# Wide projections, attention outcome in groups of four query tiles, and the recurrence's values by way of DRAM, in a one-core hybrid block

## The chip, the cores and the metric

The kernel runs on one core of one Trainium2 chip. The metric is the device time of one execution in microseconds, from a few runs of the same kernel; lower is better. The change is looked at against the kernel before, run on the same chip.

## What is computed

One layer of a streaming encoder on 1024 tokens of width 1024, all in float32. Cut to what matters here:

```python
h = rmsnorm(x, norm_mix_g)
z = h @ w_in                                   # one projection, cut into:
(hq, hf, hi, hg, fq, fk, fv, ff, mq, gate_logits) = split(z)
y_a = hgrn2(hq, hf, hi, hg)                    # gated recurrence, 4 heads of 128, chunks of 64
y_b = fox(fq, fk, fv, ff)                      # attention, 8 heads of 64, causal, with forget bias
y_c = memory(mq, rmsnorm(mem) @ mem_kv_w)      # attention into 256 memory tokens, 4 heads of 128
gates = sigmoid(gate_logits)                   # one gate per branch and channel
merged = sum(gates[b] * (y @ w_br[b]) for b, y in enumerate((y_a, y_b, y_c)))
x = x + merged @ w_out
h2 = rmsnorm(x, norm_ffn_g)
a, v = split(h2 @ w_up)                        # 2 x 2816
x = x + (gelu(causal_conv3(a)) * v) @ w_down

# fox, per head and block of 128 queries, over all keys s <= t:
s = q_hat @ k_hat.T / 8 + F[t] - F[s]          # F: running sum of log forget gates
y = softmax(s) @ v                             # q_hat, k_hat: normed per head
```

## The kernel before, in words

**Precision.** Every product is made of three float32r matmuls (`mm3`, L158 to L162): a factor is split into a high part (a cast, L166) and the rest (a difference, L174), and high x high, high x low and low x high are added in PSUM. The attention's products with their own split operands use two (L924/L925 for the logits, L965/L966 for the outcome).

**Order of the work.** Nearly everything is laid out so that TensorE always has a matmul at hand. The program is written as generators that `weave` interleaves, and `ahead` gives the attention's and the recurrence's steps a higher priority, so that the scheduler takes other work ("fill") only where they are not ready. The order of each engine's instructions is fixed when the program is built; at run time an engine works through its own list and waits by semaphores. DMAs are issued from the queues of SyncE (SP) and of GpSimd (POOL), each in its order.

The stages by the span's time: norm and the normed input `uh`/`ul` (high and low), the dense units (gates, memory queries) up to about 212 us; values and keys/queries of the first attention pair, and the attention into memory, to 325; the forgetting attention to about 681; the recurrence (HGRN) to 895 with the branch of the attention; the other two branches to 980; output projection to 1070; channel mixer up to 1475 and its down projection to the end.

**The attention** has 4 pairs p of 2 heads i; head h is 2p + i. `fox_proj(p)` computes keys and queries of a pair by `token_major` (L704): 8 token tiles of 128, each one PSUM bank of which 256 columns are used, so 8 x 3 matmuls of 128x256 per tile (L160 to L162, `pp`). They go to a tile `z`, get their norm (squares, a reduction, a power on POOL) and are transposed by `fox_prep`. `fox_attn(p, i)` (L901) makes a head: it loads the head's forget bias as a row of 1024 to all partitions (`nf`, SP queue, L909), and takes query tiles two by two. For each query tile tb: logits (`lg`, two PSUM banks, up to 1024 keys), on DVE the bias added and the row maximum taken (L930; the diagonal tile with the masked bias `nfm` from POOL), small steps (L935 to L941), on ACT the exponential with its sum (L940), on POOL the scaling by the inverse sum (L942). Then the outcome of two query tiles: for each pair of key tiles the probabilities are transposed on PE (L953, L954, L956) into one of two banks `tr`, cast on ACT to `ph` (L166), the rest on DVE to `pl` (L174), and multiplied with the split values `vhl` (L965, L966) into `po`, of which 256 columns are used. `po` is evacuated by ACT and DVE to `yp` and stored (L969 to L971).

**The fill** beside each head: keys and queries of the next pair beside i = 0, gate chunks (`gates_early`) beside i = 1 (3, 3 and 3 of them by `NFOX`, one more beside the last pair), and the recurrence's values (`hgrn_values`, L1012) in two halves of 256 columns beside the last two heads, evacuated directly to `Vf`, which held the attention's values before. Behind the attention comes `hgrn_prep(0)`: six halves of 512 columns (`cm_chunk`), each evacuated by DVE (L1046) to a gate tile and on to the tiles of the recurrence. The scheduler takes it, too, between the last heads' steps.

**Buffers.** PSUM: three banks `pp` for projections, two `lg`, two `tr`, one `po`. Weights come to `raw` (2 buffers) and are split to `wh`, `wl` (3 buffers each). A gate tile is 128x512, from a small ring. The attention's row tiles `pt` have 4 buffers of 128x1024, which the squares of the key norm use as well.

## Time and profile before

| | us |
|---|---|
| runs of the kernel before | 1698.56, 1699.6, 1700.24 (median 1699.6) |
| profiled execution | 1700.23 |
| its span, first to last instruction | 1698.4 |
| PE busy | 1691.0 |
| DVE busy | 1150.8 |
| ACT busy | 800.9 |
| POOL busy | 324.6 |
| mean granted TensorE clock | 0.999 of full |

The profiled execution is one run; its span is what the rows of the profile add up to, and 1.8 us lie around it. A row such as `pp<-uh,wh 128x512 x205 | 80.9, 395` is a group of like instructions: how many, busy time and mean ns of one. Matmuls overlap in PE's pipeline, so that the distance of their starts is shorter than their length. In the timeline a row gives start, length, engine, line and tile. In the table of windows, each row gives the window, its length, then the busy time (and count) of PE, of PE's weight load, DVE, ACT and POOL, the granted clock, the DMA share and GB/s.

### The profile page before, as it was taken

Reading aid. Unit: us, or ns where it says so; the run is one execution under the profiler, and the core shown is the slowest. Engines: PE = TensorE matmul, PEld = TensorE weight load, DVE = VectorE, ACT = ScalarE, POOL = GpSimd, SP = SyncE. Lnnn points to the kernel's source line nnn. Section 1 sums busy time; section 2 is a strip of 40 time slices with the busy share of each in tenths; the row PEclk is TensorE's granted clock in tenths of the full one; section 3 lists DMA queues with packets and bytes.
Section 4 is the critical chain, followed back from the end, with each engine's and each line's share of the span. In section 5 each row is a group of like instructions: output and inputs, shape, how many; then the busy total and the mean of one; then the engine's idle time right before and its main releaser. Section 6 shows DMA issues by size and latency. Waiting matters only on the chain.

```text
span 1698.4 us, 24291 instructions
## 1 busy us (share of the span) xinstructions
PE 1691.0 (100%) x8957; PEld 1452.4 (86%) x8957; DVE 1150.8 (68%) x2057; ACT 800.9 (47%) x1428; POOL 324.6 (19%) x420
## 2 busy tenths in 40 slices
PE   9999999999999999999999999999999999999999
PEld 7888899989898998888888888888888888888887
DVE  6966455666666664886856845987878888775654
ACT  6734455545454553775631333644434444533432
POOL 0200032543433331544310000311111111100000
PEclk9999999999999999999999999999999999999999
DMA  9443232221212111110346542566544344494772
GB/s 367 157 161 106 88 139 68 77 92 51 94 59 77 63 46 57 67 32 13 106 127 209 167 186 100 165 174 169 158 139 138 118 149 143 172 363 145 251 269 87
DMA packets 83062, 227.16 MB, mean 134 GB/s; under 512 B 9712, under 2 KB 12408, under 8 KB 82816
## 3 DMA queue, kind: packets, MB, share of 16 engines
q1 hardware_dynamic: 64320, 160.54, 26.8%
q0 software_dynamic: 18048, 64.50, 13.2%
q8 instruction: 70, 1.15, 0.3%
q10 hardware_dynamic: 576, 0.59, 0.1%
q14 instruction: 48, 0.39, 0.1%
HBM read 180.72 MB, written 67.93 MB: 146 GB/s over the span
## 4 chain that ended last, share of the span: by engine, by line
PE 99%; DVE 0%; ACT 0%; DMA 0%; issue 0%; ACTq 0%; DVEq 0%
PE pp L160 21%; PE pp L162 21%; PE pp L161 21%; PE lg L160 4%; PE lg L162 4%; PE lg L161 4%; PE tr L162 3%; PE tr L161 3%; PE tr L160 3%; PE po L966 1%; PE lg L925 1%; PE lg L924 1%; PE po L965 1%; PE po L160 1%; PE po L161 1%; PE po L162 1%
## 5 line engine op out<-in xcount | busy, mean ns | idle before, releaser
L160 PE MATMUL pp<-uh,wh 128*128 128x512 f32 x412 | 163.3, 396 | 0.0
L161 PE MATMUL pp<-ul,wh 128*128 128x512 f32 x412 | 162.9, 395 | 0.0
L162 PE MATMUL pp<-uh,wl 128*128 128x512 f32 x412 | 162.5, 394 | 0.0
L161 PE MATMUL pp<-wl,uh 128*128 128x256 f32 (+1 forms) x512 | 146.3, 286 | 0.0
L162 PE MATMUL pp<-wh,ul 128*128 128x256 f32 (+1 forms) x512 | 146.1, 286 | 0.0
L160 PE MATMUL pp<-wh,uh 128*128 128x256 f32 (+1 forms) x512 | 145.6, 286 | 0.0
L166 ACT CAST wh<-s 128x512 fp32r<-128x512 f32 x110 | 66.5, 621 | 131.6 <-PE pp L161 55.1
L166 ACT CAST wh<-raw 128x1024 fp32r<-128x1024 f32 (+2 forms) x76 | 67.6, 890 | 100.6 <-PE pp L161 86.2
L166 ACT CAST wh<-rw 128x512 fp32r<-128x512 f32 x87 | 53.2, 619 | 108.1 <-PE pp L161 70.2
L160 PEld LDWEIGHTS pp<-wh,uh 128*128 128x128 f32 x512 | 97.3, 190 | 1.2
L161 PEld LDWEIGHTS pp<-wl,uh 128*128 128x128 f32 x512 | 97.4, 190 | 1.0
L162 PEld LDWEIGHTS pp<-wh,ul 128*128 128x128 f32 x512 | 97.4, 190 | 0.9
L1457 POOL DMA_DIRECT2D rw<-in_w_up x44 | 24.1, 555 | 372.4 <-DVE wl L1350 171.3
L166 ACT CAST dwh<-wr 128x1024 fp32r<-128x1024 f32 (+1 forms) x41 | 40.2, 980 | 115.8 <-PE tr L161 40.0
L162 PEld LDWEIGHTS pp<-uh,wl 128*128 128x128 f32 x412 | 77.5, 188 | 15.1
L174 DVE TENSOR_TENSOR wl<-raw,wh 128x1024 fp32r<-128x1024 f32 (+2 forms) x75 | 78.0, 1040 | 17.8 <-ACT wh L166 17.6
L160 PEld LDWEIGHTS pp<-uh,wh 128*128 128x128 f32 x412 | 77.5, 188 | 14.6
L161 PEld LDWEIGHTS pp<-ul,wh 128*128 128x128 f32 x412 | 77.5, 188 | 14.5
L940 ACT ACTIVATE pt<-pt,st 128x128 f32<-128x128 f32 (+3 forms) x64 | 49.7, 777 | 41.7 <-DVE st L937 33.9
L174 DVE TENSOR_TENSOR dwl<-wr,dwh 128x1024 fp32r<-128x1024 f32 (+1 forms) x41 | 46.3, 1129 | 31.7 <-ACT dwh L166 31.7
L942 POOL TENSOR_SCALAR pt<-pt,st 128x128 f32<-128x128 f32 (+3 forms) x64 | 49.1, 767 | 78.4 <-DVE st L941 64.1
L1350 DVE TENSOR_TENSOR wl<-rw,wh 128x512 fp32r<-128x512 f32 x69 | 47.7, 704 | 22.7 <-PE pp L162 18.2
(500 smaller groups left out, 5123.2 us busy)
## 6 DMA issues: line engine op xcount, KB each, us to landing
rw<-in_w_up POOLq DMA_DIRECT2D x44, 512.0 KB, 4.7
sd<-in_w_dn POOLq DMA_DIRECT2D x30, 512.0 KB, 6.0
br<-yd SPq DMA_DIRECT2D x30, 512.0 KB, 5.0
raw<-in_w_cm SPq DMA_DIRECT2D x24, 512.0 KB, 3.4
gd<-gt SPq DMA_DIRECT2D x48, 256.0 KB, 2.0
gt<-gd SPq DMA_DIRECT2D x48, 256.0 KB, 2.7
yd<-fc SPq DMA_DIRECT2D x44, 256.0 KB, 2.2
wr<-sd SPq DMA_DIRECT2D x20, 512.0 KB, 4.5
```

The source lines that it names most:

```text
L160: PE.matmul(ps, lh, rh, start=first, stop=False, skip_group_check=more)
L161: PE.matmul(ps, lh, rl, start=False, stop=False, skip_group_check=more)
L162: return PE.matmul(ps, ll, rh, start=False, stop=last, skip_group_check=more)
L166: return S.copy(out, in_)
L174: return (sub or V).tensor_sub(l, src, h.bitcast(F32))
L924: PE.matmul(ps[:, :w], qa[i][:, tsl], kh[i][:, s0:s0 + w], start=True, stop=False)
L925: fox_sets[p][3] = PE.matmul(ps[:, :w], qa[i][:, tsl], kl[i][:, s0:s0 + w], start=False, stop=True)
L940: S.activation(pt[:, :ns], pt[:, :ns], AF.Exp, bias=st[:, 2:3], accum_out=st[:, 3:4])
L942: G.tensor_scalar(pt[:, :ns], pt[:, :ns], st[:, 3:4], 0.0, ALU.mult, ALU.add)
L965: PE.matmul(o, vhl[:, sb, :], ph[:, src], start=(sb == 0), stop=False)
L1350: late["split"] = V.tensor_sub(l, src, h.bitcast(F32))
L1457: late["raw"] = G.dma_start(raw[:, 2 * i:2 * i + 2, :], src[:, 2 * i:2 * i + 2, :])
```

## The change

1. **Keys and queries of pairs 2 and 3 in one wide projection.** `fox_proj_late` projects 512 columns at a time (both pairs), evacuates them to a gate tile and stores them to DRAM (`zd`); `fox_load` loads each pair's part to `z` and does its norm. `w_late` replaces the last two parts of `w_fqk`.
2. **The recurrence's values** are projected 512 columns wide too and stored to DRAM (`hid`); 8 loads bring them to `Vf` behind the attention's last use of it.
3. **Outcome by groups of four query tiles.** For each key tile, up to four transposes fill one bank `tr`; one cast, one difference, and two matmuls of up to 512 columns. Row tiles `pt` are one tile per query tile, of the length it needs.
4. **Fill**: beside the heads now: pair 1's projection, 3 gates with one half of the wide projection, the other half with the load of pair 2, gates, load of pair 3, one gate and half of the values, the other half of the values.
5. **Squares in a tile of their own**, in halves.
6. **The last outcome's evacuation** (`fox_out` of head 7, group 1) is issued behind the third of the evacuations of `hgrn_prep(0)`, into a gate tile.
7. `wh` and `wl` have 4 buffers. The memory branch's eight loads (`yc`) are issued one by one through branch 0, each behind a small POOL instruction (`warm`) that reads a gate tile. In the channel mixer two loads move from POOL's queue to SP's, and two wait for POOL's differences. The program is built with a smaller DMA scratch (2048).

```diff
-NFOX = [0, 3, 0, 3, 0, 3, 1]
+NFOX = 10
+WIDE = 4
...
-            hl = [wp.tile([P, 4 * 264], F32R, tag=t, name=t, bufs=3) for t in ("wh", "wl")]
+            hl = [wp.tile([P, 4 * 264], F32R, tag=t, name=t, bufs=WIDE) for t in ("wh", "wl")]
...
-            w = [weights(src[q], (4, ncol)) for q in range(2)]
+            per = 2 if ncol == HB else 4
+            w = [weights(src[q], (per, ncol)) for q in range(KC // per)]
...
+    def fox_norm(z):
+        zz = z.rearrange("p b (h d) -> p (b h) d", d=64)
+        r = cp.tile([P, 16], F32, tag="fr", name="fr", bufs=2)
+        for i in range(2):
+            sq = pq.tile([P, 8, 64], F32, tag="fsq", name="fsq")
+            S.activation(sq, zz[:, 8 * i:8 * i + 8, :], AF.Square)
+            V.reduce_sum(r[:, 8 * i:8 * i + 8], sq, axis=AX.X)
+        rstd_small(r, r, 64)
+        V.tensor_mul(zz, zz, r.unsqueeze(2).to_broadcast([P, 16, 64]))
...
+    def fox_proj_late():
+
+        def evac(tb, ps):
+            t = gate_tile()
+            S.activation(t, ps, AF.Copy, scale=rt[:, tb:tb + 1])
+            SP.dma_start(zd[tb], t)
+
+        yield from token_major(w_late[0], HB, evac)
+
+    def fox_load(p):
+        cs = slice((p - 2) * 256, (p - 1) * 256)
+        for n in range(2):
+            z = fox_tile(p, n)
+            SP.dma_start(z, zd[4 * n:4 * n + 4, :, cs].rearrange("b p c -> p b c"))
+            fox_norm(z)
+            yield
...
+    def fox_out(yp, po, dst):
+        S.copy(yp, po[64:128, :])
+        V.tensor_add(yp, po[0:64, :], yp)
+        SP.dma_start(dst, yp)
...
-        for tp in range(4):
+        for g in range(2):
...
-                pt = pf.tile([P, T], F32, tag="pt", name="pt", bufs=4)
+                pt = pf.tile([P, ns], F32, tag=f"pt{tb}", name=f"pt{tb}")
...
-            for sp in range(tp + 1):
+            for sb in range(4 * g + 4):
                 ptr = ps_tr()
...
+                first = max(sb - 4 * g, 0)
+                for j in range(first, 4):
+                    PE.transpose(ptr[:, j * P:(j + 1) * P], pts[j][:, sb * P:(sb + 1) * P], ident)
...
+                c = slice(first * P, HB)
+                split(S, ph[:, c], pl[:, c], ptr[:, c])
+                PE.matmul(po[:, c], vhl[:, sb, :], ph[:, c], start=sb == 0, stop=False)
+                PE.matmul(po[:, c], vhl[:, sb, :], pl[:, c], start=False, stop=sb == 4 * g + 3)
...
+            if (h, g) == (7, 1):
+                late["tail"] = po, ybd[a, p, g * HB:(g + 1) * HB]
+                return
...
+    late_proj = fox_proj_late()
+    first = (fox_proj(1), chain(islice(late_proj, 4), fox_load(2)), gates_early(2))
+    second = (chain(gates_early(1), islice(late_proj, 4)), gates_early(3), gates_early(3))
     for p in range(3):
-        weave((ahead(fox_attn(p, 0), AHEAD), FOX_STEPS), (fox_proj(p + 1), 8))
+        weave((ahead(fox_attn(p, 0), AHEAD), FOX_STEPS), (first[p], (8, 6, 4)[p]))
         fox_prep(p + 1, fox_sets[p][3])
-        weave((ahead(fox_attn(p, 1), AHEAD), FOX_STEPS), (gates_early(NFOX[2 * p + 1]), 2 * NFOX[2 * p + 1], FOX_LATE))
+        weave((ahead(fox_attn(p, 1), AHEAD), FOX_STEPS), (second[p], 6, FOX_LATE),
+              *([(fox_load(3), 2, 0.1)] if p == 1 else []))
+    run_all(late_proj)
...
-        for pc in range(2):
-            def evac(tb, ps, pc=pc):
-                S.activation(Vf[:, tb, pc * 256:(pc + 1) * 256], ps, AF.Copy, scale=rt[:, tb:tb + 1])
-            yield from token_major(w_hi[pc], 256, evac)
+        def evac(tb, ps):
+            t = gate_tile()
+            S.activation(t, ps, AF.Copy, scale=rt[:, tb:tb + 1])
+            SP.dma_start(hid[tb], t)
+        yield from token_major(w_late[1], HB, evac)
...
-        weave((ahead(fox_attn(3, i), AHEAD), FOX_STEPS), (islice(values, 8), 8),
-              (gates_early(0 if i else NFOX[6]), 2 * NFOX[6], FOX_LATE))
+        weave((ahead(fox_attn(3, i), AHEAD), FOX_STEPS), (chain(gates_early(1 - i), islice(values, 4)), 6 - 2 * i))
     run_all(values)
+    for tb in range(8):
+        SP.dma_start(Vf[:, tb, :], hid[tb])
...
-    run_all(hgrn_prep(0))
+    for i, _ in enumerate(hgrn_prep(0)):
+        if i == 2:
+            fox_out(gate_tile()[:64, :], *late.pop("tail"))
...
-    for c in range(4):
-        for t, d in zip(yc, ycd):
-            with tc.issue_after(state["norm"].ins):
-                G.dma_start(t[c], d[:, c, :].bitcast(F32R))
-    run_all(branch(0, yh, yl))
+    for i, _ in enumerate(first_branch):
+        if i % 3 and i < 12:
+            p, c = i % 3 - 1, i // 3
+            mark = G.tensor_scalar(warm, late["gates"][:, 0:1], 1.0, 0.0, ALU.mult, ALU.add)
+            with tc.issue_after(mark.ins):
+                G.dma_start(yc[p][c], ycd[p][:, c, :].bitcast(F32R))
```

How this moves instructions, at three places. The first is PE's list at the end of head 7, the last of the attention (`po_7171` before, `po_6680` after: its last outcome bank; `pp_...`: banks of projections; `tr_...`: transposed probabilities). Before, a projection half of the recurrence (`pp_7501`) stands between and behind the outcome matmuls:

```order
L161 MATMUL pp_7501<-ul1_82,wh_7468 128x512
L162 MATMUL pp_7501<-uh1_81,wl_7469 128x512
L160 MATMUL pp_7501<-uh2_83,wh_7468 128x512
L965 MATMUL po_7171<-ph_7229,vhl_6260 128x256
L161 MATMUL pp_7501<-ul2_84,wh_7468 128x512
L162 MATMUL pp_7501<-uh2_83,wl_7469 128x512
L160 MATMUL pp_7501<-uh3_85,wh_7468 128x512
L966 MATMUL po_7171<-pl_7230,vhl_6260 128x256
```

After, the same place of PE's list, the last rows of the outcome and the next projection (`pp_7083`):

```order
L980 MATMUL tr_6774<-ident_72,pt7_6662 128x128
L986 MATMUL po_6680<-pl_6759,vhl_6002 128x512
L985 MATMUL po_6680<-ph_6768,vhl_6002 128x384
L980 MATMUL tr_6783<-ident_72,pt7_6662 128x128
L986 MATMUL po_6680<-pl_6769,vhl_6002 128x384
L985 MATMUL po_6680<-ph_6777,vhl_6002 128x256
L986 MATMUL po_6680<-pl_6778,vhl_6002 128x256
L985 MATMUL po_6680<-ph_6785,vhl_6002 128x128
L986 MATMUL po_6680<-pl_6786,vhl_6002 128x128
L161 MATMUL pp_7083<-uh0_79,wh_7079 128x512
```

No projection stands between these; the last one ahead of `pp_7083` stands 110 rows earlier, in the outcome of head 6.

The second place is ACT's list there. Before (`ph_...`: casts of the outcome; `gt_...` to `ha_0`, `hq_0`: the recurrence's first evacuations, tanh):

```order
L166 CAST ph_7229<-tr_7224 128x512
L166 CAST ph_7241<-tr_7237 128x384
L969 COPY yp_7249<-po_7171 64x256
L1048 ACTIVATE ha_0_7336<-gt_7368 128x512
L1048 ACTIVATE ha_0_7336<-gt_7397 128x512
L1048 ACTIVATE hq_0_7335<-gt_7432 128x512
L166 CAST wh_7839<-raw_7837 128x1024
L1048 ACTIVATE hq_0_7335<-gt_7461 128x512
```

And after, ACT's list at the same place:

```order
L167 CAST ph_6777<-tr_6774 128x256
L167 CAST ph_6785<-tr_6783 128x128
L1076 ACTIVATE ha_0_6858<-gt_6890 128x512
L1076 ACTIVATE ha_0_6858<-gt_6919 128x512
L1076 ACTIVATE hq_0_6857<-gt_6954 128x512
L928 COPY gt_6958<-po_6680 64x512
L1076 ACTIVATE hq_0_6857<-gt_6987 128x512
L1076 ACTIVATE hz_0_6991<-gt_7023 128x512
```

The copy of the last outcome bank now stands behind three evacuations of the recurrence, and these stand behind the last cast of the outcome, as before.

The third place is SP's queue around the load of head 7's bias row. Before:

```order
L971 DMA ybd_196<-yp_6341 64x256
L971 DMA ybd_196<-yp_6484 64x256
L909 DMA nf_6816<-negFd_1808 128x1024
L971 DMA ybd_196<-yp_6587 64x256
L185 DMA raw_7551<-in_w_cm 128x1024
```

After, with the loads of the recurrence's values (`Vf<-hid`) around it:

```order
L1264 DMA Vf_1789<-hid_5998 128x512 x5
L940 DMA nf_6458<-negFd_1808 128x1024
L1264 DMA Vf_1789<-hid_5998 128x512 x3
L930 DMA ybd_196<-yp_6161 64x512
L186 DMA raw_7808<-in_w_cm 128x1024
```

Five of the eight value loads now stand ahead of the bias row of head 7.

More of the change, by code (lines that the diff above doesn't have):

```diff
@@ L1287, in branch @@
                 gts.append(gt)
+            late["gates"] = gts[0]
             for n, ps in br_chunk(br, j, yh, yl):
@@ L1504, in families @@
                 for k in range(4):
-                    late["last"] = family_block(name, k, quarters(k)[q], G if name == "B21" and k > 1 else None)
+                    sub = G if name == "B21" and k > 1 else None
+                    late["pool" if sub else "last"] = family_block(name, k, quarters(k)[q], sub)
             if name == "T3":
```

75 lines of the change are left out of this document (27 added, 48 removed).

## The prediction

> **What bounds the kernel now.** I read the page's summary first, then the chain that ended last, the waits of PE, the timeline where fill and attention meet, the durations by form in the attention, and last the order of both kernels' instructions. The page's busy times:
>
> ```profile
> PE 1691.0 (100%) x8957; PEld 1452.4 (86%) x8957; DVE 1150.8 (68%) x2057; ACT 800.9 (47%) x1428; POOL 324.6 (19%) x420
> PE 99%; DVE 0%; ACT 0%; DMA 0%; issue 0%; ACTq 0%; DVEq 0%
> ```
>
> PE is busy for 1691.0 of 1698.4 us, and the chain lies on PE for 99%. PE's waits, all of them:
>
> ```profile
> PE lg L160 <- ACT uh L349: 1.8, 1, 1.8
> PE tr L265 <- POOL dull L263: 1.0, 1, 1.0
> PE po L1189 <- DVE St L1195: 0.7, 1, 0.7
> PE pp L162 <- DVE wl L1350: 0.2, 1, 0.2
> ```
>
> They come to 3.7 us, and none lies in the attention. So only two things can move the time: PE's own work, and new holes in it. A PE row's length is no price, since matmuls overlap; the price is the distance from start to start. First and last of 20 intervals each (256 wide in the memory stage, 512 wide in the channel mixer), then transposes, then 15 intervals of 512-wide fill beside the attention's end:
>
> ```profile
> 290.01 0.28 PE L160 MATMUL pp<-wh,uh 128*128 128x256 f32 x1
> 292.40 0.28 PE L162 MATMUL pp<-wh,ul 128*128 128x256 f32 x1
> ...
> 1200.04 0.39 PE L162 MATMUL lg<-T1h,wl 128*128 128x512 f32 x1
> 1204.58 0.39 PE L161 MATMUL lg<-T1l,wh 128*128 128x512 f32 x1
> ...
> 666.19 0.27 PE L954 MATMUL tr<-ident,pt 128*128 128x128 f32 x1
> 666.63 0.27 PE L954 MATMUL tr<-ident,pt 128*128 128x128 f32 x1
> ...
> 681.09 0.40 PE L160 MATMUL pp<-uh,wh 128*128 128x512 f32 x1
> 684.50 0.39 PE L160 MATMUL pp<-uh,wh 128*128 128x512 f32 x1
> ```
>
> That is 0.120 us for 256 columns, 0.227 for 512 (also in the last pair, 3.41/15), and 0.11 for a transpose (0.44/4).
>
> **The change, part by part.** *Wide projections.* 768 matmuls of 256 columns (keys and queries of the last two pairs, recurrence values) become 384 of 512: 768 x 0.120 = 92.2 against 384 x 0.227 = 87.2, so -5.0 us. PE is the bound there, so all of it counts.
>
> [...]
>
> *Outcome in groups of four query tiles.* The attention's outcome matmuls by form (this row; the one for the low halves has 128 too, and 32 of each kind are 128 wide):
>
> ```profile
> L965 PE MATMUL po<-ph,vhl 128*128 128x256 f32 x128 | 34.2, 285 | 0.0
> ```
>
> The columns stay the same (256 x 256 + 64 x 128 = 73,728 before); after, 96 matmuls have 512, and 32 each have 384, 256 and 128. With 0.175 for 384 (between 256 and 512) and 0.08 for 128 (from the two starts that follow here), before is 256 x 0.120 + 64 x 0.08 = 35.8, after 96 x 0.227 + 32 x (0.175 + 0.120 + 0.08) = 33.8: -2.0. The end of the attention before:
>
> ```profile
> 679.71 0.22 PE L965 MATMUL po<-ph,vhl 128*128 128x128 f32 x1
> 679.76 0.28 PE L966 MATMUL po<-pl,vhl 128*128 128x128 f32 x1
> 679.82 0.19 PEld L161 LDWEIGHTS pp<-ul,wh 128*128 128x128 f32 x1
> 679.88 0.45 PE L161 MATMUL pp<-ul,wh 128*128 128x512 f32 x1
> ...
> 680.35 1.15 ACT L1048 ACTIVATE ha<-gt 128x512 f32<-128x512 f32 x2
> 681.02 1.29 DVE L1046 TENSOR_TENSOR gt<-pp,rx 128x512 f32<-128x512 f32 x2
> ...
> 697.42 0.60 PE L1174 MATMUL tr<-ident,kE 128*128 128x128 f32 x4
> ```
>
> *The fill runs out.* Before, a projection matmul starts 0.12 us behind the last outcome matmul and stood between the outcome's steps up to there. After, PE's order has 110 matmuls in a row without one: head 6's last eight outcome steps and nearly all that is left of head 7. By the distances above they are 16.3 us of PE work. All six halves of the recurrence's first projection are already done by then, three in gate tiles and three in PSUM; the next one (pp_7083) needs the bank of pp_6962, whose DVE step needs a gate tile that ACT frees by a tanh queued behind head 7's last split. So in this stretch PE waits for DVE, ACT and POOL with nothing else to do. Their prices in the attention:
>
> ```profile
> L174 DVE TENSOR_TENSOR pl<-tr,ph 128x512 fp32r<-128x512 f32 x48 | 32.2, 684 | 12.0 <-ACT ph L166 11.8
> L930 DVE CUSTOM_DVE_ANT_0 pt<-lg,nf 128x512 f32<-128x512 f32 x32 | 22.0, 689 | 20.8 <-PE lg L925 10.8 <-PE tr L953 9.7
> L930 DVE CUSTOM_DVE_ANT_0 pt<-lg,nfm 128x128 f32<-128x128 f32 x64 | 18.2, 285 | 13.2 <-POOL nfm L919 7.0 <-PE lg L925 2.8 <-PE po L965 2.0
> L937 DVE TENSOR_SCALAR st<-st 128x1 f32<-128x1 f32 x56 | 11.6, 207 | 0.8
> L941 DVE RECIPROCAL st<-st 128x1 f32<-128x1 f32 x64 | 10.3, 160 | 27.4 <-ACT pt L940 26.8
> L166 ACT CAST ph<-tr 128x512 fp32r<-128x512 f32 x48 | 27.1, 588 | 24.9 <-PE tr L954 16.9 <-PE po L965 7.4
> L940 ACT ACTIVATE pt<-pt,st 128x1024 f32<-128x1024 f32 x8 | 9.2, 1150 | 10.2 <-DVE st L937 10.2
> L940 ACT ACTIVATION_READ_ACCUMULATOR pt<-pt,st 128x1 f32 x64 | 12.0, 188 | 0.0
> L942 POOL TENSOR_SCALAR pt<-pt,st 128x1024 f32<-128x1024 f32 x8 | 9.0, 1123 | 19.0 <-DVE st L941 12.8 <-PE tr L956 6.2
> ```
>
> I walked the four queues in the new order with such rows (narrower forms from the same view), 0.04 us from one engine to another, and DVE instructions overlapping by 0.07 (681.02 above: two took 1.29). (1) To the end of the logits: splits, logits reductions and small steps on DVE are 14.8 us against 10.9 on PE; PE loses **3.7**. (2) The last block's softmax, 0.207 + 1.150 + 0.188 + 0.160 + 1.123 = 2.8 and a small maximum, follows its last reduction; PE has about 1 us left beside it, and loses **1.9**. (3) The last eight outcome steps: four transposes 0.44, 0.16 until the last has ended, cast 0.588, difference 0.684 and crossings are about 1.95 for one of two transposed banks, so about 1.0 a step where PE works 0.44 + 0.45 = 0.89; the first shows its whole cast and difference. **2.4**. (4) Behind the last split, the DVE step that frees the bank of pp_7083: **0.9**. With 0.3 of crossings the sum is **9.2**. Below, nothing is lost if each is overlapped better than the walk has it (0); above, the same rows one behind another, DVE's 14.8 and then (2) to (4) with no PE work beside them, leave about 14. I keep 9.2, as it uses each row once in the queue's order.
>
> *Start of the recurrence.* Before, 77 fill matmuls cover the step from the last outcome matmul to the transposes at 697.42; after it is 53, 53 x 0.227 = 12.0 us. The last outcome's copy, sum, store and one more gate tile lie ahead of this stage's work, some 12.7: **+0.7** (0 to 2).
>
> *At no cost.* DMA traffic by way of DRAM for the late keys, queries and values hides behind the fill:
>
> ```profile
> gd<-gt SPq DMA_DIRECT2D x48, 256.0 KB, 2.0
> gt<-gd SPq DMA_DIRECT2D x48, 256.0 KB, 2.7
> nf<-negFd SPq DMA_DIRECT2D x8, 512.0 KB, 3.7
> ych<-ychd POOLq DMA_DIRECT2D x4, 512.0 KB, 8.0
> ycl<-ycld POOLq DMA_DIRECT2D x4, 512.0 KB, 9.6
> ```
>
> Store and load together are 4.7 us, and a head's time separates them. Without that cover a key pair would be late by at most those 4.7. The branch's eight loads, paced over its first 12 of 16 steps, have four steps (48 matmuls, 10.9 us) for the last to land in 9.6; missed, it costs the rest of that load, up to 5. Squares in their own tile, one accumulator for the outcome, later loads in the channel mixer and the smaller DMA ring lie off PE's chain: 0 each, with at most 0.2 to gain at the one wait there (L162 <- L1350) and one landing of 4.7 to lose.
>
> Sum: -5.0 - 2.0 + 9.2 + 0.7 = **+2.9**. The profiled execution took 1700.23 us (span 1698.4 and 1.8 around it), so 1703.1; the runs' median, 1699.6, is 0.6 lower, so **1702.5**.
>
> **The rivals.** *B, the clock falls in the thin stretch.* Two windows near the start (PE busy after the first comma, granted clock third from last):
>
> ```profile
> 4.00:7.00 3.00, 1.21 (x7) 0.70 (x6) 1.46 (x7) 1.99 (x5) 0.00 (x0) 1.00 1.04 383
> 7.00:10.70 3.70, 3.70 (x11) 2.88 (x11) 3.03 (x7) 2.25 (x6) 0.00 (x0) 0.54 1.03 396
> 640.00:681.00 41.00, 41.00 (x219) 34.94 (x218) 18.64 (x51) 13.83 (x27) 6.46 (x10) 1.00 0.17 56
> ```
>
> Behind 3.0 us in which PE was busy 1.21 came 3.7 us at 0.54. The new stretch has 16.3 us of work in 25.5, 0.64 busy, and single holes up to 1.9 us; before, PE had no hole there (last row). It decides once a window comes as empty as that first one. One such window costs 3.7 x 0.46 = 1.7; two to four, since holes recur to the end of the stretch, give +3.4 to +6.8: 1706 to 1709, middle **1707.5**. Against it: PE is busier here than in the first window.
>
> [...]
>
> *C, the cover is not lost.* DVE runs ahead, because reductions of head 7 that need no fill are done early, and (1) goes: 9.2 - 3.7 = 5.5, with the other parts overlapped to 4: -7.0 + 4.0 + 0 = -3.0, **1696.6**. For it: DVE was busy only 18.64 of 41.0 us there. Against: in the new order its 14.8 us stand between those PE rows.
>
> *D, the widening does not pay*, and 512 among attention matmuls is no cheaper than two of 256: -2.0 + 9.2 + 0.7 = +7.9, **1707.5**. Against it: the last pair above, 0.227 beside the attention. [...]
>
> *E, the loads of the values delay head 7's bias row.* SP has five of them ahead of it. It is free until 7 us behind head 6's last reduction; five loads of 2.7 and its own 3.7, part in turn, could be 8 to 11: +1.4 to +4 and the sum 1704 to 1706.5, **1705.5**. That the change doesn't do what it says is part of D.
>
> **How the numbers follow.** The forecast A has 0.40 (own range 1699.5 to 1705.5), B 0.18, C 0.24, D 0.08, E 0.10. Measurement can tell about 0.2%, here 3.4 us: faster is below 1696.2, slower above 1703.0. A splits into 0.24 within and 0.16 above, C into 0.16 below and 0.08 within; B, D and E lie above. Faster 0.16, same 0.32, slower 0.52. The range takes in C's better half (1694) and B's upper end (1709).
>
> **What would show it.** Right: PE shows waits for DVE, ACT and POOL of 8 to 10 us in all, within 30 us of the last outcome matmul and nearly none elsewhere; the stretches ahead are 7 us shorter; the granted clock stays 1.00. A clock under 1 there is B; waits under 5 us are C; a distance of 0.24 at 512 columns is D; a wait of the head's first logits for the bias row is E. I am wrong above all if the order's stretch without fill is bridged by something that I took to be late, or if the holes feed on into the recurrence.

## The result, and the profile after

The changed kernel takes 1710.88 us (median of 6 runs, 1709.22 to 1712.61), the kernel before, run beside it, 1699.71 (6 runs, 1698.56 to 1700.24): 1.0067 times as long, interval 1.0054 to 1.008. The forecast was 1702.5 with a range of 1694 to 1709. The profiled execution took 1710.62 us, its span is 1708.8, 10.4 more than before.

The page of the changed kernel, busy times and shares of the chain that ended last:

```profile
PE 1691.2 (99%) x8445; PEld 1425.9 (83%) x8445; DVE 1156.1 (68%) x2065; ACT 796.4 (47%) x1420; POOL 331.9 (19%) x426
PE 95%; DVE 2%; issue 1%; ACT 1%; POOL 1%; DMA 1%; ACTq 0%; POOLq 0%
```

PE has 512 matmuls fewer and is as long busy as before. That is no contradiction, since a row's length is no fixed price: 512 columns wide it is 0.39 us in the stream, 0.50 as the first behind a wait (687.75 below), and 0.63 at half clock (run 9 below). The chain no longer lies on PE for 99%. PE's waits in the changed kernel (in total, times, longest):

```profile
PE tr L980 <- POOL pt L972: 1.7, 1, 1.7
PE tr L162 <- DVE B21l L175: 1.6, 1, 1.6
PE lg L161 <- ACT uh L350: 1.5, 1, 1.5
PE pp L161 <- DVE gt L1074: 1.1, 1, 1.1
PE pp L161 <- ACT wh L167: 1.1, 1, 1.1
PE tr L266 <- POOL dull L264: 1.0, 1, 1.0
PE po L985 <- DVE yp L929: 0.9, 1, 0.9
```

With the smaller ones they are 13.7 us, against 3.7. Two families are new: those at the attention's end (L972, L1074, L929) and two at the channel mixer's start (B21l, and the cast `wh` for the weights). The table of windows, before, for the attention's end, the recurrence's start and the mixer's start:

```profile
655.00:690.00 35.00, 35.00 (x178) 29.63 (x177) 16.63 (x32) 12.67 (x20) 9.51 (x7) 1.00 0.21 70
690.00:722.00 32.00, 32.00 (x174) 26.91 (x173) 27.04 (x40) 24.83 (x59) 17.26 (x13) 1.00 0.14 48
1066.00:1112.00 46.00, 45.82 (x218) 38.08 (x217) 43.72 (x71) 28.70 (x49) 14.49 (x18) 1.00 0.65 179
```

The same windows of the changed kernel, with two short ones inside the first:

```profile
655.00:690.00 35.00, 29.20 (x150) 21.65 (x149) 25.30 (x86) 21.38 (x45) 13.95 (x20) 0.95 0.19 60
676.00:679.00 3.00, 0.93 (x3) 0.39 (x3) 1.42 (x3) 1.37 (x3) 2.05 (x3) 1.00 0.28 59
679.00:683.00 4.00, 3.99 (x17) 3.29 (x18) 1.42 (x3) 1.17 (x2) 0.00 (x0) 0.57 0.32 91
690.00:722.00 32.00, 31.08 (x163) 25.27 (x162) 25.55 (x37) 25.29 (x56) 16.83 (x13) 1.00 0.18 62
1066.00:1112.00 46.00, 42.17 (x197) 33.80 (x196) 39.32 (x62) 27.68 (x47) 11.86 (x15) 1.00 0.50 152
```

PE stands idle for 5.8, 0.9 and 3.8 us where it had been idle for 0, 0 and 0.2. And from 679 to 683 the granted clock is 0.57, after three microseconds in which PE was busy for 0.93: 4.0 x 0.43 = 1.7 us.

Idle time is not the whole loss: from 655 to 690 PE is idle for 5.8 us, but the distances between its starts come to 10.0 us more than usual, the slow clock left out. So from here on a **hole** is the distance between two matmul starts beyond the usual distance of that form. Summed by hundreds of microseconds and taken against before, holes and slow clock cost +11.1 from 600 to 700, +1.3 from 700 to 800, -0.8 from 800 to 900, +4.7 from 1000 to 1200, and 0.3 at most elsewhere: +16.3. By the same distances the matmuls are 6.3 us less work. That gives +10.0 of the 10.4. How the difference divides into work and holes hangs on what is called usual: with the median distance of each width it is 8.0 us less work and 18.3 more holes. The sum stays near 10, and the two places stay.

The end of the attention, PE's timeline in the changed kernel:

```profile
674.90 0.63 PE L980 MATMUL tr<-ident,pt 128*128 128x128 f32 x4
677.23 0.44 PE L980 MATMUL tr<-ident,pt 128*128 128x128 f32 x2 [1.70 <-POOL pt L972]
678.29 0.49 PE L985 MATMUL po<-ph,vhl 128*128 128x512 f32 x1 [0.62 <-ACT ph L167]
...
686.30 0.33 PE L986 MATMUL po<-pl,vhl 128*128 128x128 f32 x1
687.75 0.50 PE L161 MATMUL pp<-uh,wh 128*128 128x512 f32 x1 [1.12 <-DVE gt L1074]
```

The first is the wait for the last block's softmax (hole 1.86), the last row the hand-over to the recurrence (hole 1.36). Between 655 and 690 the holes are 11.7 us, the slow clock (1.7) included: 4.4 ahead of the wait at 677.23, 1.9 at it, 3.9 from there to the hand-over with the slow clock in them, and 1.5 at the hand-over.

### The profile page after: what moved, and what is told of

It reads as the page before. It is cut to its first block, busy times and chain, and to the rows that moved or that the text cites. A ratio compares the mean times of both kernels' runs of the same rounds, so it can differ in the third digit from the quotient of the medians.

```text
span 1708.8 us, 23273 instructions
## 1 busy us (share of the span) xinstructions
PE 1691.2 (99%) x8445; PEld 1425.9 (83%) x8445; DVE 1156.1 (68%) x2065; ACT 796.4 (47%) x1420; POOL 331.9 (19%) x426
## 4 chain that ended last, share of the span: by engine, by line
PE 95%; DVE 2%; issue 1%; ACT 1%; POOL 1%; DMA 1%; ACTq 0%; POOLq 0%
PE pp L161 20%; PE pp L163 20%; PE pp L162 20%; PE lg L161 4%; PE lg L163 4%; PE lg L162 4%; PE tr L161 3%; PE tr L163 3%; PE tr L162 3%; PE tr L980 2%; PE po L161 1%; PE po L163 1%; PE po L162 1%; PE po L986 1%; PE lg L955 1%
## 5 line engine op out<-in xcount | busy, mean ns | idle before, releaser
L162 PE MATMUL pp<-ul,wh 128*128 128x512 f32 x412 | 162.9, 395 | 0.0
L161 PE MATMUL pp<-wh,uh 128*128 128x256 f32 (+2 forms) x384 | 123.7, 322 | 0.0
L162 PE MATMUL pp<-wl,uh 128*128 128x256 f32 (+2 forms) x384 | 123.6, 322 | 0.0
L163 PE MATMUL pp<-wh,ul 128*128 128x256 f32 (+2 forms) x384 | 123.5, 322 | 0.0
L161 PEld LDWEIGHTS pp<-uh,wh 128*128 128x128 f32 x412 | 77.5, 188 | 16.2 <-DVE gt L1074 1.3
L162 PEld LDWEIGHTS pp<-ul,wh 128*128 128x128 f32 x412 | 77.6, 188 | 14.6
L163 PEld LDWEIGHTS pp<-wh,ul 128*128 128x128 f32 x384 | 72.8, 190 | 5.3
L162 PEld LDWEIGHTS pp<-wl,uh 128*128 128x128 f32 x384 | 72.9, 190 | 5.0
L161 PEld LDWEIGHTS pp<-wh,uh 128*128 128x128 f32 x384 | 72.8, 190 | 4.9
L167 ACT CAST ph<-tr 128x512 fp32r<-128x512 f32 (+1 forms) x96 | 43.2, 479 | 66.8 <-PE tr L980 65.1
L175 DVE TENSOR_TENSOR pl<-tr,ph 128x512 fp32r<-128x512 f32 (+1 forms) x96 | 51.0, 551 | 21.4 <-ACT ph L167 20.8
L972 POOL TENSOR_SCALAR pt<-pt,st 128x128 f32<-128x128 f32 (+3 forms) x64 | 53.6, 839 | 55.3 <-DVE st L971 47.8
```

Of the source, the lines that this page charges most:

```text
L161: PE.matmul(ps, lh, rh, start=first, stop=False, skip_group_check=more)
L162: PE.matmul(ps, lh, rl, start=False, stop=False, skip_group_check=more)
L163: return PE.matmul(ps, ll, rh, start=False, stop=last, skip_group_check=more)
L167: return S.copy(out, in_)
L175: return (sub or V).tensor_sub(l, src, h.bitcast(F32))
L972: G.tensor_scalar(pt, pt, st[:, 3:4], 0.0, ALU.mult, ALU.add)
```

## The experiments

Theory F holds the missing projections at the attention's end for the cause there. Theory L says that item 7 of the change, four weight buffers and the mixer's later loads, costs the time at the mixer's start. Their rival is an echo: the mixer is late only because of what came before. All kernels here leave the computation as it is. "Mixer holes" are the holes in the 45 to 50 us behind the output projection: 0.6 in the kernel before, 5.4 in the changed one. A window of half clock counts in them with its 1.7 us; where a profile has one there, the tables give the holes without it as well.

### Item 7 on the kernel before (1 to 3)

```diff
-    ... bufs=3) for t in ("wh", "wl")]            # 1, 2: all five places
+    ... bufs=4) for t in ("wh", "wl")]
+    ... dynamic_dma_scratch_size=2048)            # 1, 2
+            with tc.issue_after(late["pool"].ins) if after else nullcontext():      # 1, 3
+                late["raw"] = (SP if begun else G).dma_start(...)
```

> The kernel before with only two edits of the change: four weight buffers instead of three (with the smaller DMA scratch that makes the room), and the channel mixer's loads as in the change (first unit's on SP's queue, second unit's behind POOL's differences). TensorE's list from the attention branch to the end is then that of the changed kernel. Theory L (these two edits alter the order of the lists at the mixer's start, and that costs the 4.8 us which the changed kernel loses between 1067 and 1110 us): span 1698.4 + 4.8 = about 1703, with TensorE's holes at that place 5.4 us in all against 0.6 before. Rival E (the mixer's loss is an echo of the attention's delay or of the other loads by way of DRAM): 1698 to 1699, holes 0.6 as before.

> The kernel before with four weight buffers and the smaller DMA scratch alone. The order of the mixer's first matmuls changes a little: the 16 small transposes of the norm stand 23 places earlier. Theory L divides its 4.8 us between this and the loads: here only the hole ahead of those transposes, 0.7 to 0.9, so a span near 1699.2; holes of 1.0 to 1.6 at the mixer's start. If the buffers are the larger part: 1701 to 1703. Rival E: 1698.4.

> The kernel before with only the channel mixer's loads as in the change (SP's queue for the first unit, the second unit's behind POOL's differences), three buffers. Theory L, loads as the larger part: +3 to +4.5, span 1701.5 to 1703. If the buffers are the larger part: 1698 to 1699.5. Rival E: 1698.4.

| | median us | ratio to before | mixer holes us | without half clock |
|---|---|---|---|---|
| 1 buffers and loads | 1705.54 | 1.0035 (1.0022 to 1.0048) | 5.4 | 5.4 |
| 2 buffers alone | 1706.77 | 1.0039 (1.0024 to 1.0054) | 7.1 | 5.4 |
| 3 loads alone | 1701.45 | 1.0009 (1.0 to 1.0019) | 1.3 | 1.3 |

The first run's holes are those of the changed kernel one by one (0.84, 1.73, 1.13, 0.45, 0.37 against 0.84, 1.74, 1.27, 0.42, 0.37), with the attention as before. The echo is out, and theory L stands. The buffers are the larger part: alone they bring 5.4 us of holes as well, and a window of half clock behind the largest of them (2.6 at 1083.58). The smaller DMA scratch, which runs 1 and 2 share, is not the cause: run 7 below has it with three buffers, and its mixer holes are 0.55.

### The mixer's start in the changed kernel (4, 6, 9, 10, 13, 14, 15)

ACT's timeline there, before:

```profile
1066.02 2.18 ACT L166 CAST B22h<-x 128x512 fp32r<-128x512 f32 x4
1068.10 0.58 ACT L1422 COPY fe<-lg 128x512 f32<-128x512 f32 x1
1068.58 2.18 ACT L166 CAST T3h<-x 128x512 fp32r<-128x512 f32 x4
1072.29 0.59 ACT L1422 COPY fe<-pp 128x512 f32<-128x512 f32 x1 [1.53 <-PE pp L162]
```

And in the changed kernel, 5.5 us later in the program's time:

```profile
1073.22 0.59 ACT L1456 COPY fe<-lg 128x512 f32<-128x512 f32 x1 [1.61 <-PE lg L163]
1073.71 2.18 ACT L167 CAST B22h<-x 128x512 fp32r<-128x512 f32 x4
1077.78 0.59 ACT L1456 COPY fe<-pp 128x512 f32<-128x512 f32 x1 [1.89 <-PE pp L163]
1078.26 2.18 ACT L167 CAST T3h<-x 128x512 fp32r<-128x512 f32 x4
...
1091.00 0.62 ACT L167 CAST wh<-rw 128x512 fp32r<-128x512 f32 x1 [3.87 <-DMA rw<-in_w_up]
```

B22, T3, B11 and T4 name operands of the mixer's products, h and l their high and low parts. The same instructions stand in another order. Each copy of a finished product (`fe`) now stands ahead of the casts for the next operand, and ACT waits 1.6 and 1.9 us at the copies while the casts could run. Last, ACT waits 3.9 us for the raw weights of the mixer's second unit. POOL's queue shows why, first before, then in the changed kernel:

```profile
1068.02 1.05 POOL L1457 DMA_DIRECT2D rw<-in_w_up  x2 [13.69 <-ACT B22h L166]
```

```profile
1085.13 1.43 POOL L175 TENSOR_TENSOR B21l<-x,B21h 128x512 fp32r<-128x512 f32 x1 [0.26 <-ACT B21h L167]
1086.51 1.14 POOL L1492 DMA_DIRECT2D rw<-in_w_up  x2
```

The load is issued 6.2 us behind the start of the output projection's last matmul before (1061.87), and 19.2 behind it after (1067.36). (The stage list above ends the output projection at 1070; the mixer's first products start at 1062.10.) So there are two candidates: the lists of ACT and DVE (O), and the load behind POOL's differences (R). In run 2, with the buffers alone, ACT waits the same 1.61 and 1.89 us at the copies. In run 7, with three buffers and the small scratch, the copies stand behind the casts as before. So it is the four buffers that move them. The edits:

```diff
 4   -  (SP if begun else G).dma_start(raw...)      +  G.dma_start(raw...)      # load as before, unheld
 6   -  rstd_small(rt2, ps[:, :8], D)               +  the same behind T3's differences
 9   as 6, and the copies of T1's and T2's products:
+            if name in ("B22", "T3"):
+                with tc.issue_after(late["split cast"].ins):
+                    late[name] = snap(late["xy"][name == "B22"])
 10  as 9, on the kernel of experiment 1
 13  -  (SP if begun else G).dma_start(raw...)      +  (SP if begun or after else G).dma_start(raw...), unheld
 14  9 and 13 together;   15  10 and 13 together
```

> The changed kernel with the channel mixer's loads back on POOL's queue, without the added wait. Theory L, loads as the larger part: the holes at the mixer's start fall from 5.4 to 1 to 2 us, span 1708.8 - 4 = about 1705. Rival E: 1708.8, as the attention's delay is still there.

> The changed kernel, with the second norm's DVE step in the mixer issued behind the differences of T3 instead of ahead of those of B22, and the 16 small transposes with it; everything else as in the change. Theory O (with four buffers the lists put that step first, DVE stands 3.5 us at it, and the differences behind it are late): holes at the mixer's start 5.4 to 1 to 2.5 us, span 1705 to 1706.5. Rival A (the mixer's holes come from when the weights' loads land, or from other moved rows): holes 4.5 to 5.5, span 1708 to 1709.

> The changed kernel with the lists of ACT and DVE at the mixer's start put back into the order of before: the two copies of the first products (fe) behind the casts of B22 and of T3, the norm's step behind T3's differences. In the changed kernel ACT stands 1.6 us at the first of these copies while the casts behind it could start, 4.2 us behind the output projection as before. Theory O (the order of these lists, which four weight buffers bring about, costs the holes at the mixer's start): the holes from 1066 to 1112 fall from 5.4 to 1 or 2 us, the time to about 1707. Rival P (the place of the tiles: B22 now lies over a weight buffer that is read late, so that the casts couldn't start earlier anyway): ACT waits as long at the first cast, the holes stay at 5 and the time at 1710 to 1711.

> The kernel before with four weight buffers, small DMA scratch and the moved mixer loads (first experiment: +5.8), and the copies and the norm's step put back as in the kernel of the run above. Theory O: the 4.7 us lost at the mixer's start come back and the 1.4 us gained in the memory stage stay: about 1700 to 1701. Rival P: 1705.

> The changed kernel with the raw weights of the mixer's second unit loaded from SP's queue, not from POOL's behind its differences; lists of ACT and DVE as in the changed kernel. Theory O+R (list order and this load are two causes): only the hole at B11h (1.27 us) goes, since ACT's wait of 3.87 us for the load ends earlier; the other four, 4.2 us, stay: about 1709.5. Rival R alone (the load is all of it): holes near 0.6 and 1706. Rival O alone (the list is all): 1710.9.

> The changed kernel with both: the copies behind the casts and the norm's step behind T3's differences, and the second unit's load on SP's queue. Theory O+R: the holes from 1066 to 1112 come down from 5.4 to 1 us (0.63 at T3's last difference is left), the time to about 1706.5. Rival S (the buffer of that load, which lies over the first operands, comes free only late, or DVE stands at the sum of the new weights, which comes earlier in its list): a hole of 2 us or more is left at B21 or B11, 1708.5 or more.

> The kernel before with four weight buffers and small scratch, the mixer's loads of both units on SP's queue, copies and norm's step as in the run above. Theory O+R: against the tenth experiment (1705.2) the 4.2 us of holes from 1080 on go: 1700.5 to 1701.5, with the 1.4 us gain in the memory stage kept. Rival S: 1703 or more.

| | median us | ratio to before | mixer holes us | without half clock |
|---|---|---|---|---|
| 4 loads back | 1714.34 | 1.0084 (1.0067 to 1.0101) | 6.5 | 4.8 |
| 6 norm's step later | 1711.61 | 1.0067 (1.0052 to 1.0082) | 5.05 | 5.05 |
| 9 lists put back | 1711.67 | 1.0065 (1.005 to 1.008) | 5.2 | 3.5 |
| 10 the same on experiment 1 | 1705.22 | 1.003 (1.0019 to 1.0042) | 4.95 | 3.25 |
| 13 load on SP | 1710.73 | 1.0065 (1.005 to 1.008) | 3.55 | 3.55 |
| 14 both | 1709.79 | 1.0058 (1.0043 to 1.0073) | 2.0 | 2.0 |
| 15 both on experiment 1 | 1702.38 | 1.0015 (1.0005 to 1.0024) | 1.9 | 1.9 |

Run 4 missed. With four buffers both units' loads stand on POOL behind the norm's power, and the holes without the clock fall by 0.6 us only. The run is 3.5 us slower in the median (2.9 against the kernels before that ran beside each), and its profile has two windows of half clock more than the changed kernel's, one at the attention's end and one at 1088.5: 3.4 us. Run 6 missed: with the norm's step alone the holes move to other places, and their sum stays. Run 9 missed in its sum and hit in its parts. Three of the holes (0.84, 0.42, 0.37) and the one at B21l (1.74) went, one of 0.63 came at T3, and the one at B11h grew from 1.27 to 2.62, which is the wait for the load. Behind that last one, from 1090.3 on, the clock fell to half; from ACT's waits and PE's timeline of that run:

```profile
ACT wh L167 <- DMA rw<-in_w_up: 3.9, 1, 3.9
```

```profile
1089.99 0.55 PE L161 MATMUL pp<-B11h,wh 128*128 128x512 f32 x1 [2.46 <-ACT wh L167]
...
1090.76 0.63 PE L162 MATMUL pp<-T4l,wh 128*128 128x512 f32 x1
1091.19 0.63 PE L163 MATMUL pp<-T4h,wl 128*128 128x512 f32 x1
```

And the window of that half clock, 3.4 us at 0.50:

```profile
1090.30:1093.70 3.40, 3.40 (x9) 2.67 (x8) 3.32 (x6) 0.62 (x1) 0.90 (x1) 0.50 1.01 413
```

So O alone saves 1.9 us of holes (5.4 to 3.5), and the slow clock takes 1.7 of them back; R alone (13) saves 1.85, and both (14) 3.4. The two nearly add up: they overlap by the part that went over to B11h, where the lists' gain meets the load's wait. The other runs of the kernel of run 9 show a clock of 0.997 to 0.998 as well, against 0.999 in those of the changed kernel, so its median tells little of the lists. ACT and SP in run 14:

```profile
1074.02 2.18 ACT L167 CAST B22h<-x 128x512 fp32r<-128x512 f32 x4
1076.10 0.58 ACT L1456 COPY fe<-lg 128x512 f32<-128x512 f32 x1
1086.52 0.61 ACT L167 CAST wh<-rw 128x512 fp32r<-128x512 f32 x1
```

```profile
1071.50 9.40 SPq L1492 DMA_DIRECT2D rw<-in_w_up  x4
```

No wait is left in these rows. Run 14 still missed its time: the largest hole left, 1.06 at B11h, ends with DVE's difference of the weights (`wl`), as rival S has it. On the kernel before (15 against 1) both together are worth 3.2 us in the median, as the holes say (5.4 to 1.9). On the changed kernel the median moved by 1.1 only. In the profile of run 14 there are 3.4 us less at the mixer, but 1.4 more in the first hundred microseconds and 0.8 more from 660 to 720, and run 11 below shows that medians of four runs move by as much. So the last pair of runs was made. Runs 10 and 15 missed for one more reason: the 1.4 us gain in the memory stage that they count on isn't there; the attention began at 325.25 in the profile of run 2, but at 326.8 to 327.0 in runs 1, 3 and 15, as before (326.7); the profiled runs differ by up to 3 us in their first hundred.

### The attention's end (5, 7, 8, 11, 12, 16)

```diff
 5   -NCOVER, NPAIR = 2, 10  -NFOX = 10   +NCOVER, NPAIR = 2, 8  +NFOX = 12   # two more gates as fill, late:
     -  (chain(gates_early(1 - i), islice(values, 4)), 6 - 2 * i)
     +  (chain(islice(values, 4 + 4 * i), gates_early(3 * i)), 4 + 6 * i)
 7   the kernel before, outcome by groups of four and small scratch alone
 8   the changed kernel, outcome by groups of two as before, last evacuation not moved
 11  +  with tc.issue_after(late["exp"].ins): SP.dma_start(Vf[:, tb, :], hid[tb])   # exp: ACT's
 12  9 and 11, and ha_0 allocated first in the recurrence's pool
 16  +  with tc.issue_after(late["nf"].ins): SP.dma_start(Vf[:, tb, :], hid[tb])    # nf: SP's own
```

> The changed kernel with two gate chunks taken from the dense units (there 7/8 of the work) and made as fill beside head 7. Fill within the attention goes from 241 to 263 us, TensorE's work by +2.7 us; in its list the longest stretch without a projection there shrinks from 16.2 to 6.3 us. Theory F (the attention's end waits because the fill is used up): holes there 11.7 to about 4, no fall of the granted clock, span 1708.8 - 8 + 2.7 = about 1703.5. Rival D (DVE and the softmax of the last head bind whatever stands between): holes about 10, span 1710 to 1711.5.

> The kernel before with the outcome in groups of four query tiles alone (row tiles per query tile, squares in their own tile, smaller DMA scratch for the room): projections 256 wide, three weight buffers, fill and mixer as before. Theory F: the outcome's 2.0 us are gained, as its list keeps fill nearly to the end (longest stretch without it 4.2 us): holes 1 to 2 more, span 1697 to 1698.5. Rival G (groups of four make the head's chain longer and starve TensorE at the end): holes of 8 to 10 there, span 1705 to 1707.

> The changed kernel with the outcome in groups of two query tiles as before, and its last evacuation not delayed; wide projections, four weight buffers, loads of the mixer as in the change. Theory F: the fill is as short as in the change (its list has a stretch of 14.1 us without projection), so holes of 8 to 12 stay at the attention's end and 5.4 at the mixer's start; +2.0 of work: span 1708 to 1711. Rival G: the holes at the attention's end go, span 1700 to 1702.

> The changed kernel with the eight loads of the recurrence's values issued behind the last exponential of the attention, so that none stands ahead of head 7's bias row on SP's queue. Theory E (the bias row, 6.15 us under way instead of 3.7, makes head 7's logits late, and that costs a part of the holes at the attention's end): the row lands 2.4 us earlier, the holes from 655 to 690 fall by 1 to 2.4 us and the time to 1708.5 to 1710. Rival: DVE has other work until then and head 7's logits wait for PE and DVE's own list: the holes stay within 0.4 us, 1710.5 to 1711.

> The changed kernel with the copies and the norm's step put back, the value loads late, and the recurrence's first tile (ha_0) placed over tiles that are dead by then instead of over the bias row and row tiles of the attention, so that its evacuations could start earlier. If the three act apart: 1710.9 - 4 - (0 to 2) - (0 to 1), 1704 to 1707. Theory F (TensorE's list has 110 matmuls without a projection at the attention's end, whatever frees the tiles): no more than 0.5 us of the holes from 655 to 720 go by the tile's place. Rival H (the hand-over waits for that tile): 1 to 2 us of the holes from 685 to 720 go.

> The changed kernel with head 7's bias row ahead of all eight value loads on SP's queue (before, five stood ahead of it). Theory E: the row lands 2.4 us earlier and the holes from 655 to 690 fall by 1 to 2.4 us: 1708.5 to 1710. Rival: those holes come from the missing projections alone and stay within 0.5 us: 1710.4 to 1711.4.

| | median us | ratio to before | holes and slow clock 660 to 720 |
|---|---|---|---|
| changed kernel | 1710.88 | 1.0067 | 13.9 |
| 5 two more gates, late | 1710.65 | 1.0062 (1.0047 to 1.0077) | 10.2 |
| 7 groups of four on before | 1718.46 | 1.0111 (1.0094 to 1.0128) | 8.9 |
| 8 groups of two | 1714.26 | 1.0086 (1.0071 to 1.0102) | 14.7 |
| 11 value loads tied to ACT | 1712.69 | 1.0071 (1.0054 to 1.0088) | 14.6 |
| 12 lists, 11 and tile moved | 1711.1 | 1.0064 (1.0049 to 1.0079) | 15.2 |
| 16 bias row first | 1710.98 | 1.0066 (1.0049 to 1.0082) | 13.9 |

The kernel before has 1.2 in the last column.

**Run 8** keeps the wide projections and takes the groups back: the holes stay, and the stretch of PE's list without a projection is still 14.1 us. So the groups of four are not needed for them; run 8 agrees with theory F for the wide projections. **Run 5** missed its time. It shortens that stretch from 16.2 to 6.3 us of PE work; the holes fall by 4.7 us from 660 to 680, but rise by 1.2 from 680 to 700, and by the distances the two gates are 2.7 us more work as fill than in the dense pairs. From 655 to 690 there are 6.1 us of holes left of 11.7, where theory F asked for 4 and rival D for 10, and the clock stays at 1.00. So fill put back takes about half of the loss there. The largest holes left end with ACT's cast of the outcome (1.34) and at the hand-over (1.34). **Run 7** missed by far. The window in which its attention hands over, and its waits:

```profile
682.50:685.50 3.00, 0.47 (x5) 0.33 (x3) 2.05 (x3) 2.98 (x5) 0.84 (x1) 1.00 0.01 3
685.50:690.00 4.50, 4.08 (x11) 3.21 (x12) 1.45 (x3) 1.32 (x3) 4.40 (x4) 0.62 0.77 233
```

```profile
PE pp L160 <- DVE gt L1287: 9.1, 1, 9.1
PE pp L160 <- DVE gt L1040: 3.0, 1, 3.0
```

9.1 us of it lie in the first branch, where a gate's load stands on SP's queue behind the loads of x, and the half clock behind that wait costs 2.4 more; that is a list that this edit drew, and says nothing on the change. Without the two the run would take about 1707, still 7 us more than the kernel before and near what rival G had, 1705 to 1707. Its longest stretch without a projection is 4.2 us, and still 3.0 us go at the hand-over, 1.5 at the recurrence's first transposes and 1.7 to the clock. At the hand-over ACT's list has a weight cast, for which ACT waits 3.56 us, ahead of the recurrence's evacuations (L1042, from 683.93), and behind these comes the DVE step for which PE waits:

```profile
682.37 1.05 ACT L166 CAST wh<-raw 128x1024 fp32r<-128x1024 f32 x1 [3.56 <-PE pp L161]
685.19 1.27 DVE L1040 TENSOR_TENSOR gt<-pp,rx 128x512 f32<-128x512 f32 x2
```

So from 660 to 720 the wide projections alone lose as much as both (14.7 against 13.9), and the groups alone 8.9; the two don't add up. Theory F does not say why the groups alone lose, and it stays open whether that has a part in the changed kernel.

**Run 11** told nothing. The loads stand on SP's queue and the edit ties them to an ACT instruction, so their order stayed; it is the changed kernel once more. Against the kernel before it is 12.4 us slower, the changed kernel 11.2: medians of four to six runs differ by that much. Run 12 missed its 1704 to 1707; with the tile moved and the edits of 9 and 11, it shows the same holes (1.34 at the hand-over) and three slow windows, one of them at the mixer: rival H is out. **Run 16** moved the loads. POOL at the first use of head 7's bias row, in the changed kernel and in run 16:

```profile
655.71 0.46 POOL L949 TENSOR_TENSOR nfm<-nf,mskf 128x128 f32<-128x128 f32 x1 [3.25 <-DMA nf<-negFd]
```

```profile
654.64 0.46 POOL L949 TENSOR_TENSOR nfm<-nf,mskf 128x128 f32<-128x128 f32 x1 [0.94 <-DMA nf<-negFd]
```

The row comes earlier and POOL waits 2.3 us less, but the holes from 665 to 690 are the same one by one (1.05, 0.56, 0.44, 1.86, 0.78, 0.50, 1.36). Theory E is out.

### The size of the mixer's part (17, 18)

Run 17 is run 5 with the mixer edit of run 14, and run 18 is run 5 once more.

> The kernel of the fifth experiment (two more gates as fill, no window of half clock) with the mixer's copies, norm's step and second load as in the fourteenth. If the holes at the mixer's start are worth what their sum says (5.4 to 2.05), it is 3.4 us faster than the run beside it: about 1707.3, against 1710.6. Rival: the holes only move the wait elsewhere (later in the mixer or the down projection), and it is 1 us faster or less: 1709.5 to 1710.5.

> The kernel of the fifth experiment once more, as the measure for the run beside it: 1710.6, mixer holes 5.4, clock 1.00 at the end of the attention.

Run 17 takes 1703.80 us (11 runs, 1703.21 to 1704.94), run 18 1710.89 (5 runs, 1709.49 to 1711.14); against before 1.0021 (1.0012 to 1.003) and 1.0062 (1.0049 to 1.0075). The difference is 7.1 us, twice the forecast. The mixer holes are 0.56 against 5.4, 4.8 less. From 660 to 720 there are 7.7 us of holes and slow clock against 10.2. The attention's holes are the same one by one up to 685. Then PE's list has nine projections earlier in run 17, though the edit lies 380 us behind that place, and run 18 had a window of half clock that run 17 had not. So the pair doesn't measure the mixer's part alone: 4.8 us of holes went where the edit is, and the rest came with the list at the attention's end. Run 17 is the fastest version with the change in it, and still 0.2% slower than the kernel before. No version here beat that.

## Why the prediction was wrong

**The step that failed** is a sentence under "At no cost": "Squares in their own tile, one accumulator for the outcome, later loads in the channel mixer and the smaller DMA ring lie off PE's chain: 0 each". The four weight buffers, which item 7 names beside them, got no term at all. Runs 1 to 3 show 4.8 us of holes at the mixer's start from this item alone, and the buffers bring them without the loads (run 2). Runs 9, 13, 14 and 15 show the two ways by which they come: the copies ahead of the casts in ACT's list (1.9 us by run 9), and the second unit's load behind POOL's differences (1.85 by run 13). The sentence named one landing of 4.7 us as the most to lose; that the size is near is chance, as no single landing makes these holes. It took the two loads for the only thing that moves, and never read ACT's list there, where the order of both kernels already differed. The wait "L162 <- L1350" that it hoped to gain from is the neighbour of the place.

**Wide projections, groups of four**: -7.0 forecast, -6.3 measured in distances (-8.0 with the median distance of each width). Two rows of the wide projection beside the attention, 11 intervals apart:

```profile
453.04 0.39 PE L161 MATMUL pp<-uh,wh 128*128 128x512 f32 x1
455.53 0.39 PE L163 MATMUL pp<-uh,wl 128*128 128x512 f32 x1
```

2.49/11 = 0.226: rival D is out.

**The fill runs out**: right in mechanism and place, and close in its parts: up to the last softmax 3.7 forecast, 4.4 measured; the softmax 1.9 against 1.86; the last outcome steps 2.4 against 2.2 without the slow clock; the hand-over 0.9 against 1.36. The sum was 9.2, and +11.1 came. The difference is mostly rival B with one window (1.7 us), which I had priced at two to four and put apart from the forecast. Its sign from the first window (1.21 of 3 us busy) was met here with 0.93, though it is no threshold, as the last section shows. Rival C (the cover is not lost) is out.

**Start of the recurrence**: +0.7 forecast, +1.3 from 700 to 800, and -0.8 behind it. The size is near by luck: at the transposes that the forecast named, now at 700.00, the hole is 0.1, and those that came are at 705.35 (0.53) and 715.29 (0.72), where PE waits for DVE. **DMA by DRAM, paced branch loads**: no PE wait stands at either; the branch's loads landed in 5.3 and 5.8 us. **Rival E**: its row was late and cost nothing (run 16).

So of the 8.4 us between forecast and median, 4.7 are the mixer's start and 1.9 the attention's end; the other 1.8 are within what the division into work and holes and the spread of the runs leave open. What stays open: why four buffers put the copies first in the list, and what the groups of four lose by themselves (run 7).

## What to carry to other kernels

Here one buffer more in a pool changed the order of ACT's list 400 us behind the place for which it was meant. So compare the lists of all engines to the end of the program, and price each place where a waiting instruction now stands ahead of work that was ready. When an edit takes one wait away, look at the next wait and at the granted clock before judging it: in run 9 the hole at B11h grew by 1.35 us, and a window of half clock behind it took 1.7, so that of 3.4 us of holes that went only 0.2 showed (0.6 came at T3). And fill that gets cheaper is fill that runs out: the change saved 6.3 us of matmuls, and the attention's end gave 11.1 back. Other work put in its place (run 5) took 3.7 us of that and cost 2.7 as fill.

## What the hardware showed

- The half clock came in pieces of 3.4 us, 1.7 us lost in each: the granted clock was 0.57 over the 4.0 us from 679 in the changed kernel, 0.50 over the 3.4 us from 1090.30 in run 9, 0.84 and 0.82 over the two stretches of 5 us from 1080 in run 2. One such window stands at the attention's end in the profile of the changed kernel and of runs 6, 7, 9, 11, 13, 14, 16 and 18, two in a row (6.8 us) in runs 4 and 12, none there in runs 5, 8 and 17. One more stands at the mixer's start in runs 2, 4, 9, 10 and 12, and three in a row (10.2 us) in and behind the 9.1 us wait of run 7.
- How empty PE is does not decide it alone. Runs 5 and 18 are the same kernel with the same holes up to 685 (0.34, 1.34, 0.28, 0.50, 0.27, 0.50, 0.34, 1.36). The windows of run 18, then of run 5:

```profile
681.00:684.00 3.00, 2.04 (x10) 1.45 (x10) 1.61 (x4) 2.21 (x6) 0.96 (x1) 1.00 0.01 3
684.00:688.00 4.00, 3.77 (x10) 3.01 (x11) 4.00 (x9) 1.35 (x3) 3.90 (x3) 0.57 0.08 19
```

```profile
684.00:688.00 4.00, 2.88 (x13) 2.27 (x14) 3.40 (x7) 2.20 (x5) 3.84 (x2) 1.00 0.01 2
```

  Run 18 fell behind 3 us with 2.04 busy, run 8 kept the full clock behind 3 us with 1.21 (687.5 to 690.5). Nor is the time always lost: run 5 waits 1.9 us for DVE at 697, where run 18, slowed just before, waits 0.4, and both lose 4.9 us from 680 to 700.
- The first hundred microseconds of a profiled run differ by up to 3 us from run to run of like kernels (3.8 to 6.9 us of holes), while most single holes of the later stages repeat to 0.1 us. A stage is therefore better compared by its own holes than by the span.
